# Moving the sums of the weights from GpSimd to VectorE beside the dilated heads and in the second w_up pair, and taking that pair's first two products earlier

## The chip, the cores and the metric

The kernel runs on one core of a Trainium2 chip. The core has five engines that run side by side, each taking its own instructions strictly in order: TensorE (PE: matmuls, with its weight loads shown as PEld), VectorE (DVE), ScalarE (ACT), GpSimd (POOL) and SyncE (SP, which here only issues DMAs). They wait for one another through semaphores. Matmul results land in PSUM, in banks of 128 x 512 floats; everything else lies in SBUF or in device memory. The metric is the device time of one execution in microseconds.

## The reference

One layer of a bidirectional encoder over 1024 sample rows and 256 prompt rows, all in float32, model width 1024:

```python
h = rmsnorm(x, g_mix)
z = h @ w_in                       # queries, keys, values of two branches, and gates
o_a = banded_attention(qa, ka, va, A_WINDOW, 1, rel_bias[:, :8], sink)
o_b = dilated_mixture(qb, kb, vb, rel_bias[:, 8:])   # 3 groups of 4 heads, dilation 1, 4, 16
merged = gates[0] * (o_a @ w_branch_a) + gates[1] * (o_b @ w_branch_b)
x = x + merged @ w_out
h = rmsnorm(x, g_mlp)
x = x + square(relu(h @ w_up)) @ w_down
y = rmsnorm(x, g_final)
```

## The kernel before

**Precision.** Every large product is made of three: each float32 operand is split into a high part (a copy rounded to fp32r, made by ACT) and a low part (operand minus high part, made by DVE, whose tile names end in `lo`), and PE adds low x high, high x low and high x high.

**Seven products for eight.** For the sample rows the projections by w_in and w_up use a Strassen-like scheme: the rows and the contraction are each halved, and so are the columns of a pair of 128-column weight tiles. Seven products (`seven`, twelve matmuls of 128x512 each) take the place of eight. The left factors are A11, A12, S2, S3, S1, A22 and S4, in this order. The right factors are four tiles: `parts[0]`, the split of `raw[0]`, for A11 and A12; `parts[1]`, the split of `ta`, for S2 and S3; `parts[2]`, the split of `tb`, for S1 and A22; `parts[3]`, the split of `raw[1]`, for S4. `ta` and `tb` hold four sums of weight quarters of 128x512 elements, each of which needs the one before it or the raw weights. The 256 prompt rows are multiplied plainly by `parts[0]` and `parts[3]` (`prompt`, 24 matmuls of 128x256).

**Preparing a pair.** `right_pair` is a generator. Step by step it issues the two loads on SP, makes the four sums on POOL (L384 to L387), and splits `raw[0]`, `ta`, `tb` and `raw[1]`, with ACT's half and DVE's half as two steps. With `late=True` the split of `raw[0]` comes ahead of the sums. Its caller decides between which products each step is put (`steps_of(nb, n)` takes the next n steps), and that sets each engine's order: in the stages concerned the instructions run in the order of the program. Tiles with the tag `w` (the weights, their parts, `ta` and `tb`) share ten slots.

**Mixed pairs.** `pair` runs the fourteen pairs of columns of w_in. From the tenth on (j = 9 to 13, `late` there) the attention of the dilated heads (`attention_b`) runs beside the products. `beside` (the function `tick`) is called about every half product and takes two or three attention steps each time: `scores` (PE, then a reduction L518 and a negation L521 on DVE, then exponentials L523 on ACT), `transposes` (PE L534, then a copy), `values_of` (PE L546, a copy, and a store issued by POOL, L550). Pairs 9 to 12 prepare a successor. They issue its loads after S2, and after S1 they take three steps at once: the sums on POOL and the two halves of the split of `raw[0]`.

**The start of w_up.** `up` runs the sixteen pairs of w_up columns. Pair 0 begins while its left factors are still being made: `entering` is advanced by `next(hooks, None)` between products and makes the splits of S3, S1 and A22, then `combine_last` (which makes S4: twice a difference L1390 on DVE, a copy on ACT and a difference L186 on DVE), then `split_prompt` (the tiles phi and plo). S4 and S1 add up in one PSUM bank, `x`: DVE has to read it (`relu2_sum`, L1698) before S4 may add to it. Pair 0 makes its two prompt products after S4, the other pairs make the first of them after A12; all use the single bank `pv`, which ACT empties (L1694, L1695). At the end of each pair POOL makes four sums of the relu outputs (L1753 to L1756), and SP stores seven tiles `u` to memory. Pair 0 takes the load of pair 1's weights after A12, the split of `raw[0]` after S1, and the sums (on POOL) after S4.

Of the kernel before, what the change touches and what calls it, by code (L numbers as in the profile page):

```python
# [15 lines left out]
P = 128  # L16
# [81 lines left out]
def encoder_kernel(  # L98
# [37 lines left out]
    def bank(tag, name=None):  # L136
        return psum.tile([P, 512], F32, name=name or tag, tag=tag, bufs={"mm": 3, "sc": 2, "pt": 2, "pv": 1}[tag])
# [182 lines left out]
    def steps_of(gen, n):  # L320
        for _ in range(n):
            next(gen, None)
# [44 lines left out]
    def right_pair(cols, out, make=wslot, late=False):  # L367
# [12 lines left out]
        if late:  # L380
            yield from part(raw[0], (P, KC, P))
        b11, b21, b12, b22 = raw[0][:, :4], raw[0][:, 4:], raw[1][:, :4], raw[1][:, 4:]
        ta, tb = make("ta", (P, 2, 4, P)), make("tb", (P, 2, 4, P))
        nc.gpsimd.tensor_tensor(tb[:, 0], b12, b11, op=ALU.subtract)  # L384
        nc.gpsimd.tensor_tensor(ta[:, 1], b22, b12, op=ALU.subtract)
        nc.gpsimd.tensor_tensor(ta[:, 0], b22, tb[:, 0], op=ALU.subtract)
        nc.gpsimd.tensor_tensor(tb[:, 1], b21, ta[:, 0], op=ALU.subtract)  # L387
        yield
        if not late:
            yield from part(raw[0], (P, KC, P))  # L390
        for src, shape in ((ta, (P, 2, 4, P)), (tb, (P, 2, 4, P)), (raw[1], (P, KC, P))):
            yield from part(src, shape)
# [419 lines left out]
    if True:  # L812
# [16 lines left out]
        class Rows:  # L829
# [5 lines left out]
            def begin(self):  # L835
                self.z = stage("long", (P, T), n=4)
# [80 lines left out]
        def pair(b, parts, cols, nxt, hooks, beside, late):  # L917
# [6 lines left out]
            nb = right_pair([w_in3[:, :, c : c + P] for c in nxt], np_) if nxt else iter(())  # L924
# [32 lines left out]
            beside()  # L957
            steps_of(nb, 3)
            next(hooks, None)
            seven(z, A22, parts[2], 1, False, mid=beside)  # L960
            one.sum(512, 512, z, c2)
            one.store()
            beside()
            next(hooks, None)
            seven(x, S4, parts[3], 1, False, mid=beside)
            two.direct(0, 512, x)
            beside()
            two.direct(NS, NP, prompt(parts[3], "mm", beside))
# [718 lines left out]
    with ExitStack() as pre:  # L1687
# [12 lines left out]

        def up(j, b, parts, hooks):

# [6 lines left out]
            x, y, z = bank("mm", "x"), bank("pt", "y"), bank("sc", "z")  # L1709
            nb = np_ = None  # L1710
            seven(x, A11, parts[0], 0, last=False)
            c1 = stage("c1", 512)
            nc.scalar.activation(c1, x, AF.Copy)
            steps_of(b, 2)
            next(hooks, None)
            seven(y, A12, parts[0], 1)
# [18 lines left out]
            nc.scalar.activation(c7, z, AF.Copy)  # L1735
            next(hooks, None)
# [71 lines left out]
```

## Time and profile before

| what | value |
|---|---|
| median of 3 runs | 1775.78 us (1774.84 to 1782.72) |
| profiled execution | 1774.43 us |
| its span, first to last instruction | 1772.7 us |
| mean granted TensorE clock | 0.993 |
| POOL sums L384 to L387 | 30 each; 39.8, 42.7, 48.4 and 52.4 us busy |

In the tables of stretches each engine has its busy time and, in parentheses, its number of instructions; PEclk is the share of TensorE's full clock that was granted. In a timeline each row has the start and the length in microseconds, then the engine, the line of the kernel, the operation, the tile written and the tiles read; brackets give how long the engine idled before, and what it seems to have waited for. The chain of waits follows the end of the execution back to its start. The mixed pairs run from about 348 to 585 us, the start of w_up lies near 970 to 1015.

### The profile page before, as it was taken

The numbers are of one execution on the slowest core, as the hardware profiler recorded it, in microseconds if no ns is written. First come the engines' busy times: TensorE is split into PE (matmuls) and PEld (weight loads), VectorE is DVE, ScalarE is ACT, GpSimd is POOL, SyncE is SP. The second block draws the span as 40 slices with busy tenths as digits, with TensorE's granted clock in tenths as the row PEclk, the third lists the DMA queues.
The fourth block names the chain that finished last, engine by engine and source line by source line (L and its number), as shares of the span: only waits on it lengthen the run. The fifth ranks groups of instructions, "written<-read, shape, count | busy, mean of one in ns | idle before, by whom it ended". The sixth has DMA issues, their size and how long they took to land.

```text
span 1772.7 us, 25231 instructions
## 1 busy us (share of the span) xinstructions
PE 1722.8 (97%) x9248; PEld 1461.3 (82%) x9248; DVE 990.1 (56%) x1683; ACT 711.5 (40%) x1531; POOL 550.5 (31%) x472
## 2 busy tenths in 40 slices
PE   7999999999999999999999899999999999999998
PEld 6898888877777899888888688888888788888886
DVE  6623323445545477576648645545454886667575
ACT  6232233344443355464336433333333433333345
POOL 0222321223322365100010355546555451305040
PEclk9999999999999999999999899999999999999999
DMA  6415335555464953185302134443345854633333
GB/s 232 146 38 164 105 112 142 138 164 151 138 169 130 286 144 97 63 273 190 132 36 99 64 126 129 152 151 117 118 146 201 296 191 149 227 101 118 120 113 119
DMA packets 214780, 256.36 MB, mean 145 GB/s; under 512 B 24887, under 2 KB 144523, under 8 KB 214528
## 3 DMA queue, kind: packets, MB, share of 16 engines
q1 hardware_dynamic: 201424, 228.26, 39.9%
q0 software_dynamic: 12144, 24.38, 4.5%
q10 hardware_dynamic: 1088, 2.10, 0.3%
q8 instruction: 73, 1.20, 0.3%
q14 instruction: 51, 0.42, 0.1%
HBM read 169.10 MB, written 90.73 MB: 147 GB/s over the span
## 4 chain that ended last, share of the span: by engine, by line
PE 60%; DVE 3%; ACT 2%; issue 1%; DMA 1%; POOL 0%; SPq 0%; ACTq 0%; DVEq 0%
PE dn L344 20%; PE mm L192 13%; PE x L344 10%; PE pv L344 5%; PE z L344 5%; PE pv L1062 2%; PE y L344 2%; PE pt L1048 1%; PE sc L1025 1%; DMA raw<-in_w_in_dram 1%; PE sc L1026 1%; DVE clo L311 1%; DVE ulo L186 0%; DVE v L1674 0%; DMA scr_g<-z 0%
## 5 line engine op out<-in xcount | busy, mean ns | idle before, releaser
L384 POOL TENSOR_TENSOR tb<-raw 128x512 f32<-128x512 f32 x30 | 39.8, 1326 | 450.0 <-PE mm L192 134.0
L344 PE MATMUL x<-chi,wlo 128*128 128x512 f32 x424 | 170.6, 402 | 7.5 <-ACT phi L185 7.3
L344 PE MATMUL dn<-dhi,ulo 128*128 128x512 f32 x448 | 174.6, 390 | 3.0 <-DVE ulo L186 3.0
L344 PE MATMUL dn<-dlo,uhi 128*128 128x512 f32 x448 | 174.3, 389 | 0.0
L344 PE MATMUL dn<-dhi,uhi 128*128 128x512 f32 x448 | 174.3, 389 | 0.0
L344 PE MATMUL x<-clo,whi 128*128 128x512 f32 x424 | 167.6, 395 | 0.1
L344 PE MATMUL x<-chi,whi 128*128 128x512 f32 x424 | 166.9, 394 | 0.0
L311 DVE TENSOR_TENSOR wlo<-ta,whi 128x1024 fp32r<-128x1024 f32 x30 | 56.6, 1888 | 187.8 <-ACT whi L309 187.8
L311 DVE TENSOR_TENSOR wlo<-raw,whi 128x1024 fp32r<-128x1024 f32 x60 | 93.9, 1564 | 103.7 <-ACT whi L309 103.7
L344 PEld LDWEIGHTS dn<-dhi,ulo 128*128 128x128 f32 x448 | 84.1, 188 | 21.3 <-DVE ulo L186 4.1
L344 PEld LDWEIGHTS x<-chi,wlo 128*128 128x128 f32 x424 | 81.0, 191 | 25.0 <-ACT phi L185 7.7
L186 DVE TENSOR_TENSOR ulo<-uraw,uhi 128x1024 fp32r<-128x1024 f32 x56 | 95.0, 1716 | 11.7 <-ACT uhi L185 11.7
L344 PEld LDWEIGHTS dn<-dlo,uhi 128*128 128x128 f32 x448 | 84.1, 188 | 17.5
L344 PEld LDWEIGHTS dn<-dhi,uhi 128*128 128x128 f32 x448 | 84.1, 188 | 17.4
L344 PEld LDWEIGHTS x<-chi,whi 128*128 128x128 f32 x424 | 80.8, 190 | 17.6
L523 ACT ACTIVATE s<-s,o 128x128 f32<-128x128 f32 (+1 forms) x120 | 52.4, 437 | 103.7 <-issue 58.3
L344 PEld LDWEIGHTS x<-clo,whi 128*128 128x128 f32 x424 | 81.0, 191 | 14.7 <-DVE clo L311 0.4
L1523 POOL TENSOR_TENSOR t<-raw,t 128x1024 f32<-128x1024 f32 x16 | 46.0, 2898 | 142.8 <-DMA raw<-in_w_down_dram 142.8
L1674 DVE TENSOR_TENSOR v<-v,dn 128x512 f32<-128x512 f32 x90 | 59.5, 682 | 43.2 <-PE dn L344 38.9
L344 PE MATMUL dn<-dhi,up 128*128 128x512 f32 x224 | 73.5, 389 | 0.0
L344 PE MATMUL pv<-phi,wlo 128*128 128x256 f32 x256 | 72.5, 283 | 0.9 <-ACT u L1694 0.9
L344 PE MATMUL pv<-plo,whi 128*128 128x256 f32 x256 | 72.6, 283 | 0.0
(332 smaller groups left out, 4785.9 us busy)
## 6 DMA issues: line engine op xcount, KB each, us to landing
scr_u<-u SPq DMA_DIRECT2D x112, 320.0 KB, 2.6
uraw<-scr_u SPq DMA_DIRECT2D x56, 512.0 KB, 4.2
raw<-in_w_in_dram SPq DMA_DIRECT2D x33, 512.0 KB, 5.4
raw<-in_w_up_dram SPq DMA_DIRECT2D x32, 512.0 KB, 5.5
raw<-in_w_down_dram SPq DMA_DIRECT2D x28, 512.0 KB, 6.4
sg<-scr_g SPq DMA_DIRECT2D x32, 256.0 KB, 5.2
uraw<-scr_u SPq DMA_DIRECT2D x28, 256.0 KB, 4.4
v<-scr_v SPq DMA_DIRECT2D x96, 64.0 KB, 2.2
```

The source lines that it names most:

```text
L186: nc.vector.tensor_tensor(lo, src, hi.bitcast(F32), op=ALU.subtract)
L192: nc.tensor.matmul(ps, a, b, start=i == 0, stop=i == len(seq) - 1)
L311: nc.vector.tensor_tensor(lo, src, hi.bitcast(F32), op=ALU.subtract)
L344: nc.tensor.matmul(ps, a, b, start=first and i == 0, stop=last and i == len(seq) - 1, skip_group_check=True)
L384: nc.gpsimd.tensor_tensor(tb[:, 0], b12, b11, op=ALU.subtract)
L523: nc.scalar.activation(s[:, h, :W], s[:, h, :W], AF.Exp, bias=nm[:, h : h + 1], accum_out=l[:, h : h + 1])
L1025: nc.tensor.matmul(ps[:, :W], q, st["k"][1][:, P * lo : P * lo + W], start=True, stop=False)
L1026: nc.tensor.matmul(ps[:, :W], q, st["k"][0][:, P * lo : P * lo + W], start=False, stop=True)
L1048: nc.tensor.transpose(ps[:, P * (i % 4) : P * (i % 4) + P], s[:, h, P * b : P * b + P], ident)
L1062: nc.tensor.matmul(pv[:, HD * h : HD * h + HD], pt[:, 2 * b + h, :], src, start=b == 0, stop=b == W // P - 1)
L1523: nc.gpsimd.tensor_tensor(o, a, b, op=ALU.subtract)
L1674: nc.vector.tensor_tensor(v, v, ps, op=ALU.add)
```

## The change

`right_pair` has a flag `vector` in place of `late`. With it, the split of `raw[0]` comes first and the four sums are made by DVE, one per step. The mixed pairs pass `late` as this flag. There the three steps after S1 are replaced by six, one at each place from after S1 to the middle of the last prompt product, each behind that place's attention steps. In w_up the flag is set for pair 1. Pair 0 takes the split of pair 1's `raw[0]` one product earlier, after S3 and so ahead of `combine_last`. It makes pair 1's products A11 and A12 (`begin`) between its own A22 and S4, and takes the four sums after S4. Pair 1 then starts from the banks that are already filled.

```diff
+        if vector:
+            yield from part(raw[0], (P, KC, P))
         ta, tb = make("ta", (P, 2, 4, P)), make("tb", (P, 2, 4, P))
-        nc.gpsimd.tensor_tensor(tb[:, 0], b12, b11, op=ALU.subtract)
-        nc.gpsimd.tensor_tensor(ta[:, 1], b22, b12, op=ALU.subtract)
-        nc.gpsimd.tensor_tensor(ta[:, 0], b22, tb[:, 0], op=ALU.subtract)
-        nc.gpsimd.tensor_tensor(tb[:, 1], b21, ta[:, 0], op=ALU.subtract)
-        yield
-        if not late:
+        for o, x, y in ((tb[:, 0], b12, b11), (ta[:, 1], b22, b12), (ta[:, 0], b22, tb[:, 0]), (tb[:, 1], b21, ta[:, 0])):
+            (nc.vector if vector else nc.gpsimd).tensor_tensor(o, x, y, op=ALU.subtract)
+            if vector:
+                yield
+        if not vector:
+            yield
             yield from part(raw[0], (P, KC, P))
...
-            nb = right_pair([w_in3[:, :, c : c + P] for c in nxt], np_) if nxt else iter(())
+            nb = right_pair([w_in3[:, :, c : c + P] for c in nxt], np_, wslot, late) if nxt else iter(())
+            def both_(n=1):
+                beside()
+                if late:
+                    steps_of(nb, n)
...
             two.sum(512, 512, x, c7)
-            beside()
-            steps_of(nb, 3)
+            both_()
+            if not late:
+                steps_of(nb, 3)
             next(hooks, None)
-            seven(z, A22, parts[2], 1, False, mid=beside)
+            seven(z, A22, parts[2], 1, False, mid=both_)
...
-            beside()
+            both_()
             next(hooks, None)
-            seven(x, S4, parts[3], 1, False, mid=beside)
+            seven(x, S4, parts[3], 1, False, mid=both_)
             two.direct(0, 512, x)
-            beside()
-            two.direct(NS, NP, prompt(parts[3], "mm", beside))
+            both_()
+            two.direct(NS, NP, prompt(parts[3], "mm", both_))
...
+        def begin(parts):
+            x, y = bank("mm", "x"), bank("pt", "y")
+            seven(x, A11, parts[0], 0, last=False)
+            c1 = stage("c1", 512)
+            nc.scalar.activation(c1, x, AF.Copy)
+            yield
+            seven(y, A12, parts[0], 1)
+            yield x, y, c1
+        begun = {}
...
+            start = begin(parts)
+            if j not in begun:
+                next(start)
+            z = bank("sc", "z")
             steps_of(b, 2)
             next(hooks, None)
-            seven(y, A12, parts[0], 1)
+            x, y, c1 = begun[j] if j in begun else next(start)
             relu2_sum(u11[:, :512], y, c1)
...
             nc.scalar.activation(c7, z, AF.Copy)
+            if not j:
+                steps_of(nb, 2)
             next(hooks, None)
...
-            if nb:
-                steps_of(nb, 3 if j else 2)
+            if nb and j:
+                steps_of(nb, 3)
             seven(z, A22, parts[2], 1, False)
             relu2_sum(u21[:, :512], z, c2)
             next(hooks, None)
+            if not j:
+                *_, begun[1] = begin(np_)
             seven(x, S4, parts[3], 1, False)
             relu2(u12[:, :512], x)
-            if not j:
-                next(nb)
             next(hooks, None)
             if not j:
+                steps_of(nb, 4)
                 prompt_out(prompt(parts[0]), (u11, u21))
```

More of the change, by code (lines that the diff above doesn't have):

```diff
@@ L365, in prompt, with right_pair @@
         return ps
-    def right_pair(cols, out, make=wslot, late=False):
+    def right_pair(cols, out, make=wslot, vector=False):
         raw = [make("raw", (P, KC, P)) for _ in range(2)]
@@ L378, in part @@
             yield from split_steps(*out[-1], src)
-        if late:
+        b11, b21, b12, b22 = raw[0][:, :4], raw[0][:, 4:], raw[1][:, :4], raw[1][:, 4:]
+        if vector:
             yield from part(raw[0], (P, KC, P))
-        b11, b21, b12, b22 = raw[0][:, :4], raw[0][:, 4:], raw[1][:, :4], raw[1][:, 4:]
         ta, tb = make("ta", (P, 2, 4, P)), make("tb", (P, 2, 4, P))
-        nc.gpsimd.tensor_tensor(tb[:, 0], b12, b11, op=ALU.subtract)
-        nc.gpsimd.tensor_tensor(ta[:, 1], b22, b12, op=ALU.subtract)
-        nc.gpsimd.tensor_tensor(ta[:, 0], b22, tb[:, 0], op=ALU.subtract)
-        nc.gpsimd.tensor_tensor(tb[:, 1], b21, ta[:, 0], op=ALU.subtract)
-        yield
-        if not late:
+        for o, x, y in ((tb[:, 0], b12, b11), (ta[:, 1], b22, b12), (ta[:, 0], b22, tb[:, 0]), (tb[:, 1], b21, ta[:, 0])):
[4 more added lines that the diff above has]
+            yield
             yield from part(raw[0], (P, KC, P))
@@ L1708, in up @@
             u11, u12, u22, u21 = u[A11], u[A12], u[A22], u[S3]
-            x, y, z = bank("mm", "x"), bank("pt", "y"), bank("sc", "z")
+            start = begin(parts)
+            if j not in begun:
+                next(start)
+            z = bank("sc", "z")
             nb = np_ = None
-            seven(x, A11, parts[0], 0, last=False)
-            c1 = stage("c1", 512)
-            nc.scalar.activation(c1, x, AF.Copy)
             steps_of(b, 2)
             next(hooks, None)
-            seven(y, A12, parts[0], 1)
+            x, y, c1 = begun[j] if j in begun else next(start)
             relu2_sum(u11[:, :512], y, c1)
```

## The prediction

> **What bounds the kernel now.** I read the page first: TensorE (PE) is busy for almost the whole span, so a gain has to come from places where it idles or is granted less than its full clock.
>
> ```profile
> span 1772.7 us, 25231 instructions
> PE 1722.8 (97%) x9248; PEld 1461.3 (82%) x9248; DVE 990.1 (56%) x1683; ACT 711.5 (40%) x1531; POOL 550.5 (31%) x472
> ```
>
> Then I asked for busy times by stretch, first over the mixed pairs (the dilated heads beside the projection products), then around the start of w_up. Columns: stretch, length, busy time of PE, PEld, DVE, ACT, POOL, granted clock (PEclk), DMA share, GB/s.
>
> ```profile
> 376.00:380.00 4.00, 2.01 (x12) 1.47 (x12) 2.39 (x2) 1.85 (x6) 3.29 (x3) 0.97 0.44 122
> 380.00:384.00 4.00, 4.00 (x16) 3.16 (x16) 3.41 (x13) 1.28 (x7) 1.29 (x3) 0.61 0.14 52
> ...
> 434.00:438.00 4.00, 3.90 (x14) 3.31 (x14) 2.05 (x7) 1.25 (x5) 0.54 (x1) 0.57 0.33 98
> ...
> 442.00:481.00 39.00, 39.00 (x281) 31.91 (x278) 19.51 (x77) 18.96 (x69) 9.07 (x16) 1.00 0.51 147
> ...
> 486.00:490.00 4.00, 2.25 (x9) 1.68 (x10) 3.56 (x14) 1.66 (x8) 2.29 (x2) 0.87 0.15 53
> 490.00:494.00 4.00, 4.00 (x19) 3.20 (x19) 0.98 (x6) 0.76 (x4) 0.98 (x2) 0.70 0.47 123
> ...
> 541.00:545.00 4.00, 4.00 (x26) 3.12 (x25) 3.00 (x11) 2.62 (x10) 0.55 (x1) 1.00 0.37 114
> ...
> 988.00:996.00 8.00, 0.99 (x2) 0.83 (x3) 6.78 (x6) 3.90 (x4) 7.31 (x4) 0.67 0.00 1
> ```
>
> PE is full in the long stretch between (442 to 481: 39.00 of 39.00 us) and empty or slow in short spots near 376, 431, 486, 538 and 990. Each of the five has a run of POOL sums in it. The timelines of POOL, DVE and PE show how the first four arise (start, length, engine, line; in brackets the idle time before).
>
> ```profile
> 376.76 1.26 POOL L386 TENSOR_TENSOR ta<-raw,tb 128x512 f32<-128x512 f32 x1
> ...
> 456.84 0.71 POOL L453 DMA_DIRECT2D bias<-wide  x1
> 457.55 0.73 POOL L454 DMA_DIRECT2D bias<-wide  x1
> ```
>
> ```profile
> 372.12 0.17 DVE L521 TENSOR_SCALAR o<-m 128x2 f32<-128x2 f32 x1
> ...
> 374.46 0.28 DVE L518 CUSTOM_DVE_ANT_0 s<-sc,bias 128x128 f32<-128x128 f32 x1
> ...
> 375.00 3.07 DVE L521 TENSOR_SCALAR o<-m 128x2 f32<-128x2 f32 x1
> ...
> 432.17 1.23 DVE L311 TENSOR_TENSOR wlo<-raw,whi 128x1024 fp32r<-128x1024 f32 x1 [2.16 <-ACT whi L309]
> ...
> 457.07 1.23 DVE L311 TENSOR_TENSOR wlo<-ta,whi 128x1024 fp32r<-128x1024 f32 x1 [1.58 <-ACT whi L309]
> ...
> 481.90 4.71 DVE L311 TENSOR_TENSOR wlo<-raw,whi 128x1024 fp32r<-128x1024 f32 x1 [0.79 <-ACT whi L309]
> ```
>
> ```profile
> 378.69 0.71 PE L534 MATMUL pt<-ident,s 128*128 128x128 f32 x2 [1.94 <-ACT s L523]
> ...
> 430.75 0.33 PE L534 MATMUL pt<-ident,s 128*128 128x128 f32 x1 [0.44 <-ACT s L523]
> ...
> 434.10 1.72 PE L546 MATMUL pv<-v,pt 128*128 128x64 f32 x8 [2.31 <-issue]
> ...
> 486.87 0.69 PE L516 MATMUL sc<-qk 64*128 64x128 f32 x4 [2.19 <-DVE m L518]
> 488.39 0.72 PE L534 MATMUL pt<-ident,s 128*128 128x128 f32 x2 [0.82 <-ACT s L523]
> ...
> 537.70 0.33 PE L534 MATMUL pt<-ident,s 128*128 128x128 f32 x1 [1.98 <-ACT s L523]
> ```
>
> A 0.17 us operation on 2 columns (L521) takes 3.07 us while POOL's sums run: it begins at 375.00 and ends at 378.07, just when POOL's third sum ends (376.76 + 1.26 = 378.02). The reduction L518, with an operand from PSUM, keeps its 0.28 us in the middle of the sums. So DVE operations that work in SBUF alone are held until POOL lets go. Behind them stand the softmax, the transposes and then PE. The 1.23 us split at 481.90 takes 4.71.
>
> **Part A: the sums beside the dilated heads.** Four mixed pairs (j = 9 to 12) prepare a successor, so 16 POOL sums become 16 DVE sums.
>
> What goes. Idle on PE: 1.94, then 0.44 + 2.31, then 2.19 + 0.82, then 1.98: 9.7 us. After three of the four, PE also runs at a low clock: 4.00 x 0.39 + 3.90 x 0.43 + 2.25 x 0.13 + 4.00 x 0.30 = 1.56 + 1.68 + 0.29 + 1.20 = 4.7 us (the clock after the fourth, 541 to 545, is 1.00). Together **14.4 us**. The 2.31 us at 434 isn't held by POOL directly: there the split at 432.17 waited 2.16 us for ACT's copy behind the late softmax, with the copy of the transposes queued behind it. After the change the ACT half and the DVE half of that split are a tick apart, so this should go too.
>
> What comes. A DVE sum of 128x512 stands in no row for SBUF operands alone; its neighbours in size do:
>
> ```profile
> 962.17 0.96 DVE L1379 TENSOR_TENSOR s<-s,hraw 128x768 f32<-128x768 f32 x1
> ...
> 970.32 0.43 DVE L1379 TENSOR_TENSOR s<-s,hraw 128x256 f32<-128x256 f32 x1
> ```
>
> Midway that is 0.69 us, or 2.8 us of DVE work per pair, in a stage where DVE is half busy (19.51 of 39). Each sum comes after its tick's attention step, one per tick. Queued behind it are the next tick's score reduction and copy of transposes, and for those PE waits. Cost between 0 and 16 x 0.69 = 11 us. The nearest row is the split at 457.07: 1.23 us, after waiting 1.58 us, in the same queue in the same sort of tick, inside the stretch in which PE lost nothing. I take 1.5 us in all, since 16 insertions will not all find a gap. ACT issues the same copies, SP the same loads at the same place; POOL's scr_b stores, which were queued behind the sums, go earlier, and nobody waits for them. Net **-12.9 us** (bounds -14.4 and -3.4).
>
> The Trainium skill, "GPSIMD Engine Reference", section "Key points", says that POOL shares its SBUF interfaces with VectorE and contends with DVE instructions in a 2-port mode or with two SBUF inputs. The sums on DVE have two SBUF inputs, so by that rule they could be held by what stays on POOL, its DMA issues. The trace has the split at 457.07, also with two, at its plain 1.23 us while POOL issued the bias loads (456.84 and 457.55), so I add nothing.
>
> **Part B: the start of w_up.** The timelines of PE and DVE and the chain of waits give:
>
> ```profile
> 987.29 0.39 PE L344 MATMUL z<-chi,whi 128*128 128x512 f32 x1
> 995.01 0.77 PE L344 MATMUL x<-chi,wlo 128*128 128x512 f32 x1 [7.34 <-ACT phi L185]
> ...
> 1004.48 0.38 PE L344 MATMUL pv<-phi,wlo 128*128 128x256 f32 x1 [0.87 <-ACT u L1694]
> ```
>
> ```profile
> 985.39 1.22 DVE L1390 TENSOR_TENSOR hraw<-hraw,s 128x1024 f32<-128x1024 f32 x1
> 987.80 1.86 DVE L186 TENSOR_TENSOR clo<-hraw,chi 128x1024 fp32r<-128x1024 f32 x1 [1.19 <-ACT chi L185]
> 989.58 2.28 DVE L1390 TENSOR_TENSOR hraw<-hraw,s 128x1024 f32<-128x1024 f32 x1
> ...
> 994.18 0.68 DVE L1698 TENSOR_TENSOR u<-x,c 128x512 f32<-128x512 f32 x1
> ...
> 1014.67 0.69 DVE L1698 TENSOR_TENSOR u<-y,c 128x512 f32<-128x512 f32 x1 [1.46 <-POOL u L1755]
> ```
>
> ```profile
> 995.01 5.46 PE x L344 x12
> 1000.47 3.16 PE pv L344 x24
> ...
> 1007.62 2.75 PE x L344 x12
> 1010.37 2.72 PE y L344 x12
> 1013.09 2.87 PE pv L344 x24
> ```
>
> PE ends A22 at 987.5 and starts S4 of the first pair at 995.01. S4 adds to bank x, which DVE must first have read (L1698 at 994.18); that read is queued behind combine_last. The ACT phi named as releaser is only what ended last by the clock. S4 then takes 5.46 us, against 2.72 for the same twelve matmuls later, and the prompt product 3.16 against 2.87: the low clock again (0.67).
>
> After the change, on the same time axis. ACT's copy of the second pair's raw[0] follows c7 (at about 984), DVE's split takes 985.4 to 986.6, so A11' and A12' run 987.5 to 993.0 without a wait. combine_last starts 1.2 us later but without POOL beside it: its two held rows fall from 1.86 and 2.28 to 1.22 each, a gain of 1.7. So bank x is free about 0.6 us earlier and S4 starts near 994.4. PE idles about 1.4 us instead of 7.34, and S4 and the prompt product run at full clock (2.74 + 0.29 saved). S4 ends near 997.1. The first prompt product waits about 0.3 for plo, which follows the two sums of relu on DVE; the 0.87 us wait for the one pv bank stays and comes a second time, since no A11' and A12' stand between the prompt products of the two pairs. S2' then starts near 997.1 + 0.3 + 3 x 2.87 + 2 x 0.87 = 1007.7, against 1015.9 now (1013.09 + 2.87): 8.2 us.
>
> Two waits come near. ta is summed by DVE (about 998.5 to 1001.2), copied by ACT after the prompt relus, split near 1007.5: just in time. And relu's sum of u11 waits for POOL's L1755 (1.46 us at 1014.67 now); POOL's chain starts only 3.6 us earlier, with the end of the pair's second prompt product (997.1 + 0.3 + 2 x 2.87 + 0.87 = 1004.0 against 1007.62), so that sum starts near 1011, the split of tb behind it ends near 1014.3, and S1', due at 1007.7 + 2 x 2.72 = 1013.1, stalls about 1.2. The next loads stand on SP behind the stores of u, which gain the same 3.6 us; they are needed a product later than the ones now, so I charge nothing. Net **-7.0 us**, bounds -4 (ta late, and a low clock on S4 after all) and -8.2.
>
> The clock bears on the 1.4 us that remain. Idle of 1.94 us was followed by 0.61 and idle of 1.98 by 1.00, so the length alone doesn't decide; 0.87 at 1004.48 cost nothing. I take no drop. The Trainium skill, "TensorE: Matmul & The Clock Gate", section "Why this matters for your kernels", asks for no idle above about 3 us. By that none of the four spots in the mixed pairs, with single idles of up to 2.31 us, should have slowed, and the sum below would be 4.7 us smaller; the clocks of 0.57 to 0.70 there say otherwise, and the rows decide.
>
> **Sum.** 12.9 + 7.0 = 19.9 us. Both stages sit between others that start from the program's order, and PE is the chain on both sides, so I carry all of it to the end. The profiled execution took 1774.43 us (span 1772.7 plus 1.7): 1774.4 - 19.9 = 1754.5. The median shown is 1775.78, 1.3 above that execution; I put the forecast at **1755**.
>
> **Rivals.**
> 1. *The wait only changes its owner in part A.* DVE's queue is in order: if each sum lands where the softmax has no slack, 0.69 us reach PE 16 times, part A nets 3.4, and the time is 1774.4 - 3.4 - 7.0 = 1764. For it: the transposes follow their scores by a tick or two. Against it: the costless 1.23 us splits. Chance 0.16.
> 2. *Part B gives little.* The pair's S2' waits for ta or S1' for tb, and S4 stays cold: 4 us or less: 1757.5 to 1761. The stalls move a few us later, because POOL's u chain and the single pv bank hold the same order. Chance 0.12, most of it inside my range.
> 3. *DVE becomes the bound beside the heads, and the kernel slower.* Each of the 16 ticks loses its 0.69 us and is followed by a low clock as near 490 (about 1.6 us): 16 x 2.3 = 36.6 against 14.4 + 7.0 saved, 15 us slower, 1790. It decides from 21.4 / 16 = 1.3 us per sum. Against it: DVE is half idle there. Chance 0.04.
> 4. *POOL is not the cause.* If PE's spots came from the pair's own order (ACT's copy ahead of the split), part A would give nothing: 1767.5. Against it: L521's ends coincide with POOL's. Chance 0.08.
>
> The forecast as worked out has 0.60. My range is 1749 (both upper bounds, 1774.4 - 14.4 - 8.2 = 1751.8, and some 3 us for shorter gaps at the same places that I did not count) to 1765 (rival 1). 0.5% is 8.9 us, about what a measurement of this kernel can tell from no change. Faster by more than that (below 1766.9): 0.60 + 0.16 + 0.12 = 0.88; within: 0.08; slower: 0.04.
>
> **What will show it.** Right: no L521 above 0.3 us and no split above 1.3 in the mixed pairs, PE busy for the whole of the four pair ends at clock 1.00; sums of about 0.69 us on DVE; A11' of the second w_up pair before S4, an idle of about 1.4 us ahead of S4, twelve S4 matmuls in 2.7 us, two gaps of 0.87 between three prompt products, and a short gap at S1'. Wrong: PE waiting for ACT's softmax or the copy of transposes just behind a DVE sum; a sum waiting for its ta or tb slot; A11' waiting for its split; or both stages shorter, and the gain lost again before the w_down stage.

## The result and the profile after

| | before | after |
|---|---|---|
| median, lowest to highest | 1776.53 us (1774.84 to 1782.72, 4 runs) | 1754.93 us (1749.7 to 1757.38, 4 runs) |
| profiled execution | 1774.43 us | 1757.38 us |
| its span, granted clock | 1772.7 us, 0.993 | 1755.6 us, 0.996 |

The ratio of after to before is 0.9869, with a 95% interval of 0.9844 to 0.9894. The forecast was 1755.0 us, with a range of 1749 to 1765. The profiled execution of after is the longest of its four, which matters further down.

The page of after, busy time by engine. POOL has 20 instructions less, DVE 20 more:

```profile
PE 1717.7 (98%) x9248; PEld 1457.8 (83%) x9248; DVE 988.3 (56%) x1703; ACT 712.6 (41%) x1531; POOL 519.8 (30%) x452
```

The stretches of after that answer to those shown of before (stretch, length, busy time of PE, PEld, DVE, ACT and POOL with counts, clock, DMA share, GB/s): the four pair ends in the mixed pairs, then the start of w_up, and one stretch at 600 that has no counterpart in the argument so far. PEclk is a mean over the stretch.

```profile
376.00:380.00 4.00, 4.00 (x25) 3.26 (x25) 3.32 (x14) 2.11 (x7) 1.31 (x3) 1.00 0.47 124
380.00:384.00 4.00, 4.00 (x28) 3.20 (x26) 2.34 (x10) 1.76 (x6) 1.78 (x3) 1.00 0.90 247
429.00:434.00 5.00, 5.00 (x36) 4.01 (x35) 3.01 (x13) 1.85 (x6) 0.54 (x1) 1.00 0.62 177
474.00:479.00 5.00, 5.00 (x30) 3.83 (x29) 4.09 (x14) 2.20 (x10) 1.01 (x2) 1.00 0.54 146
524.00:529.00 5.00, 5.00 (x31) 4.01 (x30) 3.93 (x14) 1.66 (x6) 1.08 (x2) 1.00 0.39 113
...
600.00:612.00 12.00, 9.24 (x50) 8.30 (x51) 6.05 (x20) 5.68 (x16) 4.16 (x7) 0.72 0.64 148
...
976.00:984.00 8.00, 6.34 (x29) 4.97 (x28) 5.31 (x6) 4.00 (x4) 0.00 (x0) 1.00 0.00 1
984.00:987.00 3.00, 3.00 (x14) 2.24 (x14) 2.86 (x5) 0.81 (x3) 0.00 (x0) 1.00 0.00 0
```

The four holes in the mixed pairs are closed: PE is full there, at clock 1.00. In the 8 us that end at S4 of the first w_up pair, PE now does 6.34 us of work where it did 0.99.

DVE's groups in after (count, least, median and longest ns, first and last start), with the negation that was held (L521 before, L522 now) and the first of the four sums, then DVE's timeline beside the heads and at the start of w_up (L1398 and L1706 were L1390 and L1698):

```profile
L522 DVE TENSOR_SCALAR o<-m x60: 168/170/229, 357.1 to 552.8; 128x2 f32<-128x2 f32 x60
...
L386 DVE TENSOR_TENSOR tb<-raw x5: 680/684/685, 379.9 to 988.1; 128x512 f32<-128x512 f32 x5
```

```profile
379.83 0.17 DVE L522 TENSOR_SCALAR o<-m 128x2 f32<-128x2 f32 x1
379.91 0.68 DVE L386 TENSOR_TENSOR tb<-raw 128x512 f32<-128x512 f32 x1
380.88 0.42 DVE L264 COPY pt<-pt 128x256 f32<-128x256 f32 x1 [0.29 <-PE pt L535]
...
975.58 1.22 DVE L1398 TENSOR_TENSOR hraw<-hraw,s 128x1024 f32<-128x1024 f32 x1
977.98 1.23 DVE L186 TENSOR_TENSOR clo<-hraw,chi 128x1024 fp32r<-128x1024 f32 x1 [1.19 <-ACT chi L185]
979.12 1.22 DVE L1398 TENSOR_TENSOR hraw<-hraw,s 128x1024 f32<-128x1024 f32 x1
...
982.95 0.68 DVE L1706 TENSOR_TENSOR u<-x,c 128x512 f32<-128x512 f32 x1
```

No negation takes more than 0.229 us (before: up to 3.398), a sum takes 0.68, and DVE has time to spare right behind it: at 380.88 it waits for PE, not PE for it. `combine_last` runs at its plain 1.22 and 1.23 us, where it took 1.86 and 2.28 beside POOL.

PE's timeline in after, at 602 and at the start of w_up (the idle time before a matmul in brackets):

```profile
602.76 1.11 PE L1056 MATMUL pt<-ident,s 128*128 128x128 f32 x4 [3.26 <-ACT pt L262]
...
983.78 0.47 PE L344 MATMUL x<-chi,wlo 128*128 128x512 f32 x1 [1.66 <-DVE u L1706]
...
990.77 0.39 PE L344 MATMUL pv<-phi,wlo 128*128 128x256 f32 x1 [0.87 <-ACT u L1702]
...
994.78 0.38 PE L344 MATMUL pv<-phi,wlo 128*128 128x256 f32 x1 [0.87 <-ACT u L1702]
```

S4 now waits 1.66 us instead of 7.34, and the clock behind it stays at 1.00 (984 to 987). The 0.87 us wait for the one pv bank stands there twice. The hole at 602 is new and belongs to no step of the prediction.

To see where the time went, I take four copies by ACT that both kernels make, as milestones: the copy of S3 in the last mixed pair, the copies of S2 in pairs 0 and 1 of w_up, and the copy of A11 in pair 2. First before, then after:

```profile
579.21 0.60 ACT L951 ACTIVATE c<-z 128x512 f32<-128x512 f32 x1 [1.79 <-PE z L344]
...
980.92 0.59 ACT L1728 ACTIVATE c<-x 128x512 f32<-128x512 f32 x1
...
1018.75 0.60 ACT L1728 ACTIVATE c<-x 128x512 f32<-128x512 f32 x1 [5.85 <-PE x L344]
...
1035.25 0.60 ACT L1713 ACTIVATE c<-x 128x512 f32<-128x512 f32 x1 [1.62 <-PE x L344]
```

```profile
561.33 0.60 ACT L958 ACTIVATE c<-z 128x512 f32<-128x512 f32 x1 [1.79 <-PE z L344]
...
969.97 0.59 ACT L1750 ACTIVATE c<-x 128x512 f32<-128x512 f32 x1
...
1000.95 0.60 ACT L1750 ACTIVATE c<-x 128x512 f32<-128x512 f32 x1 [3.98 <-PE x L344]
...
1018.24 0.60 ACT L1714 ACTIVATE c<-x 128x512 f32<-128x512 f32 x1 [1.62 <-PE x L344]
```

- At the end of the mixed pairs after is 17.9 us ahead. It entered them 0.24 us ahead (334.17 against 334.41 us at the copy before them), so **the mixed pairs give 17.6 us** (12.9 were forecast).
- From the second to the third milestone before takes 37.83 us and after 30.98, a gain of 6.85. The stall at S1' comes only behind that. From the second to the fourth it is 54.33 against 48.27: **the start of w_up gives 6.06 us** (7.0 were forecast). Behind it the lead stays at 17.0 us.
- Between the first and the second, in code that the change doesn't touch, the lead shrinks from 17.9 to 10.95 us: **6.9 us are lost in between**, in this execution. By the copies on the way, 4.6 of them are gone at 611, behind the hole at 602, another 1.6 near 730, and 0.7 from there to 780.

### The profile page after: what moved, and what is told of

Same layout as the page of the kernel before. It is cut to its first block, busy times and chain, and to the rows that moved or that the text cites. A ratio compares the mean times of both kernels' runs of the same rounds, so it can differ in the third digit from the quotient of the medians.

```text
span 1755.6 us, 25218 instructions
## 1 busy us (share of the span) xinstructions
PE 1717.7 (98%) x9248; PEld 1457.8 (83%) x9248; DVE 988.3 (56%) x1703; ACT 712.6 (41%) x1531; POOL 519.8 (30%) x452
## 4 chain that ended last, share of the span: by engine, by line
PE 58%; DVE 4%; ACT 2%; DMA 2%; issue 1%; POOL 1%; SPq 0%; DVEq 0%; ACTq 0%; POOLq 0%
PE dn L344 20%; PE mm L192 13%; PE x L344 9%; PE pv L344 5%; PE z L344 4%; PE pv L1070 2%; PE y L344 2%; PE pt L1056 1%; PE sc L1033 1%; DMA scr_g<-z 1%; PE sc L1034 1%; DVE clo L311 1%; DVE ulo L186 0%; DMA raw<-in_w_in_dram 0%; DMA scr_u<-u 0%
## 5 line engine op out<-in xcount | busy, mean ns | idle before, releaser
L386 POOL TENSOR_TENSOR tb<-raw 128x512 f32<-128x512 f32 x25 | 32.3, 1291 | 358.7 <-PE mm L192 134.7
L344 PEld LDWEIGHTS dn<-dlo,uhi 128*128 128x128 f32 x448 | 84.1, 188 | 17.3
L1778 POOL TENSOR_TENSOR u<-u,u 128x640 f32<-128x640 f32 x16 | 25.6, 1598 | 164.5 <-ACT u L1703 164.5
```

The lines of the kernel that those rows point to most:

```text
L344: nc.tensor.matmul(ps, a, b, start=first and i == 0, stop=last and i == len(seq) - 1, skip_group_check=True)
L386: (nc.vector if vector else nc.gpsimd).tensor_tensor(o, x, y, op=ALU.subtract)
L1778: nc.gpsimd.tensor_tensor(u[S1], u21, u22, op=ALU.add)
```

## The experiments

The theory was that of the prediction: runs of sums on POOL hold DVE, and S4 of the first w_up pair has nothing to cover its wait. Open were whether the engine or the place of the sums matters in each stage, what a sum on DVE costs, and where the 6.9 us went. The table has the first three milestones of every profiled execution: "stretch" is the time from the copy of S3 in the last mixed pair to the copy of S2 in w_up pair 0, "interval" that from there to the copy of S2 in pair 1 (the stall at S1' lies behind it). The last column has how long ACT waited for the loads of the two gate weights that it splits (L231) about 21 and 37 us behind the first milestone (30 in the kernels with earlier loads). Column 3 compares with runs of before on the same chip; products_late to sums_twice ran on another chip than the rest of the experiments.

| kernel | median us (lowest to highest, runs) | ratio to before, 95% | last copy of S3 | stretch | interval | ACT's two waits at L231 |
|---|---|---|---|---|---|---|
| before | 1776.53 (4) | | 579.21 | 401.71 | 37.83 | 2.19, 1.08 |
| after | 1754.93 (1749.7 to 1757.38, 4) | 0.9869 [0.9844, 0.9894] | 561.33 | 408.64 | 30.98 | 3.14, 4.16 |
| heads_only | 1759.16 (1756.84 to 1761.03, 4) | 0.9893 [0.9866, 0.992] | 560.75 | 406.21 | 37.71 | 2.15, 2.58 |
| wup_only | 1770.3 (1768.52 to 1771.99, 6) | 0.9959 [0.9944, 0.9974] | 579.48 | 405.02 | 30.99 | 1.84, 1.97 |
| pool_spread | 1754.71 (1754.24 to 1757.27, 4) | 0.9873 [0.9852, 0.9895] | 561.93 | 404.97 | 30.98 | 2.45, none |
| dve_old_place | 1756.14 (1753.61 to 1759.6, 4) | 0.988 [0.9856, 0.9904] | 565.09 | 403.29 | 30.99 | 2.03, 1.34 |
| products_late | 1758.78 (1754.79 to 1761.09, 4) | 0.9882 [0.9861, 0.9903] | 563.36 | 403.07 | 36.91 | 2.46, 2.15 |
| wup_pool | 1757.49 (1755.71 to 1758.49, 4) | 0.9878 [0.9863, 0.9893] | 561.75 | 402.58 | 34.43 | 2.35, 0.75 |
| early_fetch | 1749.16 (1748.78 to 1749.4, 4) | 0.9832 [0.9817, 0.9847] | 561.74 | 400.86 | 30.66 | 2.40, 0.61 |
| sums_twice | 1753.73 (1 run) | | 561.74 | 402.42 | 30.96 | 2.09, 0.95 |
| after_again | 1752.16 (1752.01 to 1756.65, 5) | 0.9863 [0.9843, 0.9882] | 561.43 | 403.36 | 30.98 | 2.65, 1.27 |
| early_again | 1751.56 (1750.47 to 1753.71, 4) | 0.9854 [0.9836, 0.9873] | 561.38 | 402.15 | 30.68 | 1.94, 0.55 |
| before_early_fetch | 1776.26 (1774.58 to 1780.45, 12) | 0.9999 [0.9989, 1.001] | 580.83 | 402.30 | 36.77 | 2.51, none |
| sums_four | 1762.43 (1 run) | | 574.79 | 400.17 | 30.95 | 2.47, 0.90 |

The runs of before beside them have medians of 1777.66 (heads_only to dve_old_place), 1778.29 (products_late to sums_twice) and 1777.42 us (the rest).

### Each part alone

`heads_only` has the mixed pairs of after and the `up` of before; `wup_only` has the mixed pairs of before and the `up` of after. (The lines of `up` that `heads_only` puts back aren't shown.)

```diff
heads_only, from after
-    def right_pair(cols, out, make=wslot, vector=False):
+    def right_pair(cols, out, make=wslot, vector=False, late=False):
...
-        if vector:
+        if vector or late:
             yield from part(raw[0], (P, KC, P))
...
-        return right_pair([w_up3[:, :, c : c + P] for c in (2 * P * j, 2 * P * j + P)], out, make, j == 1)
+        return right_pair([w_up3[:, :, c : c + P] for c in (2 * P * j, 2 * P * j + P)], out, make, False, j == 1)

wup_only, from after
-            nb = right_pair([w_in3[:, :, c : c + P] for c in nxt], np_, wslot, late) if nxt else iter(())
+            nb = right_pair([w_in3[:, :, c : c + P] for c in nxt], np_) if nxt else iter(())
...
-            both_()
-            if not late:
-                steps_of(nb, 3)
+            beside()
+            steps_of(nb, 3)
```

> Part A alone: DVE sums beside the dilated heads, w_up as before. Theory (POOL's sums hold DVE, and PE waits behind it): ACT's copy of S3 in the last mixed pair, at 579.21 us before and 561.33 in the changed kernel, comes within 1 us of 561.3, a lead of 17.6 us; no L521 above 0.3 us there. The whole gains less than that if the load-bound stretch behind the heads takes some back as it did in the profile of the changed kernel (lead 10.95 us at the start of w_up): 10 to 18 us, ratio 0.990 to 0.994. Rival (the two parts share one gain, for instance through the slots of the weights): less than 8 us.

> Part B alone: mixed pairs as before. Theory (S4 waits for the read of bank x behind combine_last, and the second pair's two products fill the wait): from the copy of S2 in pair 0 to the copy of S2 in pair 1, 37.8 us before, 31.0 in the changed kernel, here 30.5 to 31.5; the whole gains 6 to 8 us, ratio 0.996. Rival (what was won there is late again in w_down): the same 31 us, but a gain below 3 us.

Against the same runs of before, the mixed pairs alone save 1777.66 - 1759.16 = 18.5 us, a little more than the 10 to 18 expected, and the start of w_up alone saves 7.4. The milestones say the same: the mixed pairs end at 560.75 in the one and at 579.48 in the other, the interval is 37.71 and 30.99. The parts don't help or hinder each other: 25.9 us in all, and both together gave 21.6 in the first set of runs and 25.3 (after_again) in another. `wup_only` lost 3.3 us in the stretch (405.02 against 401.71) although its mixed pairs are those of before. So a loss of that size there needs no part A.

### Engine or place in the mixed pairs

`pool_spread` leaves these sums on POOL but puts them one to a tick, as after does. `dve_old_place` makes them on DVE but all at once after S1, in the place and order of before. The lines shown leave out the new parameters and a loop that repeats each sum, once here.

```diff
pool_spread, from after
-            (nc.vector if vector else nc.gpsimd).tensor_tensor(o, x, y, op=ALU.subtract)
+            (nc.vector if vector and not pool else nc.gpsimd).tensor_tensor(o, x, y, op=ALU.subtract)
...
-            nb = right_pair([w_in3[:, :, c : c + P] for c in nxt], np_, wslot, late) if nxt else iter(())
+            nb = right_pair([w_in3[:, :, c : c + P] for c in nxt], np_, wslot, late, True) if nxt else iter(())

dve_old_place, from after
-            (nc.vector if vector else nc.gpsimd).tensor_tensor(o, x, y, op=ALU.subtract)
+            (nc.vector if vector or dve else nc.gpsimd).tensor_tensor(o, x, y, op=ALU.subtract)
...
-            both_()
-            if not late:
-                steps_of(nb, 3)
+            beside()
+            steps_of(nb, 3)
```

> The changed kernel with the mixed pairs' sums back on POOL, but in the new places: the split first, then one sum in each tick. Theory (a run of sums one behind the other is what holds DVE, because POOL lets go only between separate sums): no DVE operation is held for more than about 1.3 us, the length of one sum, and most of the 17.6 us of the mixed stage stays won: lead 12 to 17.6 us at the copy of S3 of the last mixed pair. Rival 1 (any work on POOL costs DVE as much, wherever it stands): lead below 6 us. Rival 2 (only the order counted, POOL holds nothing): lead 17 to 18 us and no L521 above 0.3 us.

> The changed kernel with DVE's sums of the mixed pairs back in the old place: all four in one step after S1, then both halves of the split. Theory (the engine is what counts, the place is second): the four sums take 2.7 us of DVE at once and the split waits for ACT's copy as at 432 us before, so some of PE's idle comes back: lead 8 to 15 us at the copy of S3 of the last mixed pair, with idle of 0.5 to 2 us at each pair end. Rival (the place is what counts): lead below 4 us.

The held operation in `pool_spread`: its group on DVE, and one instance beside POOL's timeline.

```profile
L523 DVE TENSOR_SCALAR o<-m x60: 168/170/1326, 357.2 to 553.4; 128x2 f32<-128x2 f32 x60
...
386.99 0.85 DVE L523 TENSOR_SCALAR o<-m 128x2 f32<-128x2 f32 x1
```

```profile
386.49 1.31 POOL L387 TENSOR_TENSOR ta<-raw,tb 128x512 f32<-128x512 f32 x1
387.88 1.27 POOL L387 TENSOR_TENSOR tb<-raw,ta 128x512 f32<-128x512 f32 x1
```

The hold is still there: a 0.17 us negation takes 0.85 and ends at 387.84, when POOL's sum ends (386.49 + 1.31 = 387.80). POOL still makes some of these sums two in a row, but never three. So the hold now lasts at most one sum (1.326 us at the longest, against 3.398 before), and the ticks have that much to spare: the mixed pairs end at 561.93, within 0.6 us of after. In `dve_old_place` the group and the four sums on DVE are:

```profile
L522 DVE TENSOR_SCALAR o<-m x60: 169/170/235, 357.4 to 556.5; 128x2 f32<-128x2 f32 x60
...
375.46 0.68 DVE L386 TENSOR_TENSOR tb<-raw 128x512 f32<-128x512 f32 x1
...
377.38 0.69 DVE L386 TENSOR_TENSOR tb<-raw,ta 128x512 f32<-128x512 f32 x1
```

No hold is left, but 2.6 us of sums and then the split stand in a row ahead of the next score reduction. PE idles 0.27 to 0.51 us at the pair ends, less than the 0.5 to 2 expected at some of them, and the mixed pairs end at 565.09. They started 0.8 us later than in after, so the packed order costs about 3 us of the 17.6. So in the mixed pairs either half of the change is nearly enough by itself, as far as one profile of each shows. The place alone brings 17.3 us, the engine alone some 14.7. What has to go is the *run* of sums on POOL, and the move to VectorE is one way to do it.

### What a sum on DVE costs

`sums_twice` and `sums_four` issue each of the 16 sums of the mixed pairs two and four times; each ran once.

```diff
-            (nc.vector if vector else nc.gpsimd).tensor_tensor(o, x, y, op=ALU.subtract)
+            for _ in range(times):
+                (nc.vector if vector and not pool else nc.gpsimd).tensor_tensor(o, x, y, op=ALU.subtract)
```

> The changed kernel with each of the 16 sums of the mixed pairs made twice over (the same result): 16 more DVE operations of 0.69 us, two in a row in each tick. Theory (each tick has 1 to 2 us of DVE idle, so a sum costs PE nothing): the copy of S3 of the last mixed pair stays within 2 us of 561.3. Rival (DVE is near its bound there, the sums were just short enough): 5 to 11 us later.

> The changed kernel with each sum of the mixed pairs made four times over (the same result), 2.8 us of DVE work in each tick. Theory (a tick lasts about 3 us and leaves DVE 1 to 2 us): now DVE is the bound in these ticks, and the copy of S3 of the last mixed pair comes 6 to 25 us later than 561.3. Rival (DVE has more room than that): within 3 us.

Doubled, the sums cost nothing: the mixed pairs end at 561.74, against 561.33 and 561.43 in the two profiles of after. Four times as many end at 574.79, 13.5 us later than in after, of which 1.1 were there at the start of the mixed pairs (335.23 against 334.17): they cost 12.4 us, of which some 3.4 are a spell of 6.83 us at half clock that began at 494.06. DVE's and PE's timelines in `sums_four` show how:

```profile
380.50 2.86 DVE L387 TENSOR_TENSOR tb<-raw 128x512 f32<-128x512 f32 x4
```

```profile
386.74 0.91 PE L518 MATMUL sc<-qk 64*128 64x256 f32 x4 [0.80 <-DVE m L520]
```

2.86 us of DVE work in one tick is more than the tick can hide, and PE waits for a score reduction behind it. 2 x 0.69 = 1.4 us is hidden. So the slack of a tick lies between 1.4 and 2.8 us, and the 0.69 us that the change adds is free.

### The start of w_up: products or sums

`products_late` moves A11 and A12 of pair 1 back behind the prompt products, and `wup_pool` keeps the new order but makes pair 1's sums on POOL.

```diff
products_late, from after
-            if not j:
-                *_, begun[1] = begin(np_)
             seven(x, S4, parts[3], 1, False)

wup_pool, from after
-            (nc.vector if vector else nc.gpsimd).tensor_tensor(o, x, y, op=ALU.subtract)
+            (nc.vector if vector and not pool else nc.gpsimd).tensor_tensor(o, x, y, op=ALU.subtract)
...
-        return right_pair([w_up3[:, :, c : c + P] for c in (2 * P * j, 2 * P * j + P)], out, make, j == 1)
+        return right_pair([w_up3[:, :, c : c + P] for c in (2 * P * j, 2 * P * j + P)], out, make, j == 1, j == 1)
```

> The changed kernel with the second pair's first two products back behind the prompt products; the earlier split and DVE's sums stay. Theory (the two products fill the wait for bank x): the wait ahead of S4 is 6 to 7.5 us again, S4 runs at a low clock again, and from the copy of S2 in pair 0 to that in pair 1 it takes 36 to 37.5 us (31.0 in the changed kernel, 37.8 before). The whole is 5 to 7 us slower than the changed kernel. Rival (the gain came from POOL's absence beside combine_last): 31 to 33 us.

> The changed kernel with the second w_up pair's four sums on POOL, the order of all steps kept. POOL has nothing ahead of them, so they run as soon as A22 frees their slots, beside combine_last. Theory (POOL's run of sums holds DVE's operations of combine_last): two of these are stretched to 1.8 to 2.3 us again, S4 starts 1.5 to 2 us later, behind an idle of 3 to 3.6 us, perhaps at a low clock: 32.5 to 35 us from the copy of S2 in pair 0 to that in pair 1 (31.0 in the changed kernel). Rival (the engine doesn't matter here either, as it didn't among the mixed pairs once the sums were spread): 31 us.

In `products_late`, PE's first matmul of S4 and the stretch behind it:

```profile
980.23 0.76 PE L344 MATMUL x<-chi,wlo 128*128 128x512 f32 x1 [7.08 <-DVE u L1706]
```

```profile
980.00:984.00 4.00, 3.77 (x9) 3.03 (x10) 3.83 (x6) 0.57 (x1) 0.00 (x0) 0.50 0.00 0
```

Both the wait (7.08 us) and the low clock (0.50) are back, and the interval is 36.91: of the 6.85 us, 36.91 - 30.98 = 5.9 come from the place of the two products (5.1 of 6.06 if the stall at S1', which it doesn't have, is counted). In `wup_pool` these are POOL, DVE, PE and the stretch behind S4's start:

```profile
970.68 1.64 POOL L387 TENSOR_TENSOR tb<-raw 128x512 f32<-128x512 f32 x1 [92.14 <-PE z L344]
...
975.88 2.13 POOL L387 TENSOR_TENSOR tb<-raw,ta 128x512 f32<-128x512 f32 x1
```

```profile
972.35 2.30 DVE L186 TENSOR_TENSOR clo<-hraw,chi 128x1024 fp32r<-128x1024 f32 x1 [1.19 <-ACT chi L185]
974.57 2.31 DVE L1399 TENSOR_TENSOR hraw<-hraw,s 128x1024 f32<-128x1024 f32 x1
```

```profile
980.32 0.47 PE L344 MATMUL x<-chi,wlo 128*128 128x512 f32 x1 [3.83 <-DVE u L1707]
```

```profile
980.00:984.00 4.00, 3.69 (x11) 2.99 (x12) 3.83 (x6) 1.15 (x2) 0.00 (x0) 0.69 0.00 0
```

POOL has nothing else to wait for here, so its four sums come early and in one run, just beside `combine_last`, whose 1.22 us operations take 2.30 and 2.31. S4 waits 3.83 us instead of 1.66 (3 to 3.6 were expected) and the mean clock of the stretch falls to 0.69: the interval is 34.43, 3.45 more than in after. Here the engine matters, unlike in the mixed pairs. The two parts of the edit overlap, so 5.9 and 3.45 don't add up to 6.85. The whole times bear this out only in their direction: by the ratios to before, products_late is 2 to 3.5 us slower than after, where 5 to 7 were expected, and the intervals overlap.

### The time lost between the stages

In after, ACT takes the split of a gate weight (L231, 1.06 us) in the middle of the banded heads, behind the mixed pairs. If the load isn't there, everything behind it in ACT's queue waits, the copy of transposes included. First ACT's timeline in after, then in after_again:

```profile
599.97 1.06 ACT L231 ACTIVATE whi<-raw 128x1024 fp32r<-128x1024 f32 x1 [4.16 <-DMA raw<-in_w_in_dram]
...
602.13 0.57 ACT L262 ACTIVATE pt<-pt 128x512 f32<-128x512 f32 x1
```

```profile
597.47 1.06 ACT L231 ACTIVATE whi<-raw 128x1024 fp32r<-128x1024 f32 x1 [1.27 <-DMA raw<-in_w_in_dram]
```

That explains the hole at 602 in after: 4.16 us of waiting, the copy of transposes at 602.13, PE at 602.76 after 3.26 us of idling, and a clock of 0.72 over 600 to 612. `early_fetch` and `before_early_fetch` issue these loads one block earlier, in after and in before; `after_again` and `early_again` are after and early_fetch once more, with the same runs of before.

```diff
-                for t0, n in BLOCKS[::2] + BLOCKS[1:2]:
+                for part_, (t0, n) in enumerate(BLOCKS[::2] + BLOCKS[1:2]):
...
                     nc.sync.dma_start(scr_g[c][:, t0 : t0 + n], z[:, :n])
+                    if part_ == 0 and len(raws) < len(PLAIN):
+                        fetch()
```

> The changed kernel, with each load of a plain gate weight (raw) issued one block of products earlier than it is split. Theory (the stretch behind the heads gives back 3 to 7 us because ACT's copy of such a weight waits for its load, 4.16 us at 600 us in the changed kernel, with the copy of the transposes and then PE behind it): no wait of ACT for that load above 1 us, PE's idle of 3.26 us at 602 is gone, and the copy of S2 in w_up's pair 0 comes at 962 to 967 us, against 969.97. The whole gains 2 to 6 us over the changed kernel. Rival (the DMA engines are simply full there, so what comes earlier delays another load): no gain, and a wait of about the same length elsewhere between 570 and 620 us.

> The changed kernel itself once more, for its scatter. Theory (what the load-bound stretch behind the heads gives back differs from run to run with the wait for one load): the copy of S3 of the last mixed pair within 1 us of 561.3 again, but the copy of S2 in w_up's pair 0 anywhere from 962 to 970 us, and single times spread over 5 us or more. Rival (the 7 us given back belong to the change): 969 to 971 us again.

> The changed kernel with the earlier loads of the plain gate weights, again, beside the changed kernel on the same chip. Theory (that wait makes the scatter): faster than the changed kernel by 3 to 7 us, and single times within 3 us of one another. Rival (the first result was a lucky chip): no difference above 2 us.

> The kernel before with the same earlier loads and nothing else. Theory (the wait for the load is a loss of its own, smaller there since ACT waited 1.08 us and PE 0.17 us in the profile of before): 0 to 3 us faster than before. Rival (the earlier loads are worth as much without the change, so that they have nothing to do with what it gave back): 4 us or more faster.

The first result was promising, 1749.16 us and a second wait of 0.61 (the first stayed at 2.40). Repeated beside after itself it was not: 1751.56 against 1752.16 us, where 3 to 7 us had been expected, since after came out shorter this time and early_fetch longer. In before the earlier loads change nothing (0.9999, 0.9989 to 1.001). So the late load explains the hole in that one execution, but no version was shown to be better than after. The 1752.01 to 1756.65 us of after_again are a spread of 4.6 us (at least 5 were expected), and its own profile shows a stretch of 403.36 us, only 1.65 longer than that of before.

Those 1.65 us, and part of the 6.9, come from a second place. PE idles 1.91 us ahead of the transposes of `merged` in all fourteen profiles, before included. First before, then after, each with a matmul 1.2 to 1.6 us later:

```profile
742.93 0.41 PE L1162 MATMUL pt<-ident,merged 128*128 128x128 f32 x2 [1.91 <-DVE oblo L1174]
...
744.12 0.39 PE L192 MATMUL mm<-hhi,whi 128*128 128x512 f32 x1
```

```profile
729.69 0.41 PE L1170 MATMUL pt<-ident,merged 128*128 128x128 f32 x2 [1.91 <-DVE oblo L1182]
...
731.30 0.63 PE L192 MATMUL mm<-hhi,wlo 128*128 128x512 f32 x1
```

The wait is the same, but behind it before keeps its full clock, and in after matmuls of the same shape take 0.63 us instead of 0.39 for a while; that costs 1.6 us. It happens in ten of the fourteen profiles, with and without the change (wup_only and before_early_fetch have it; before, products_late, early_fetch and sums_four don't). So the profile of before was on the lucky side here, and this part of the loss can't be charged to the change.

Over all kernels the stretch takes from 400.17 to 408.64 us, with after at the top. Up to some 45 us behind the first milestone, where both waits for loads lie, the kernels part by -4.6 to +1.2 us from before; the clock behind `merged` adds 1.6 us or nothing, and up to 1.4 us are lost in smaller pieces behind it. In pool_spread the first of the two waits opened a hole in PE (1.66 us at 586.34), in heads_only and after the second. What makes a load late in one execution and not in the next was not settled.

## Why the prediction was right, and where it was not

**Mechanism of part A.** Right. The marks set out in advance are there: no held negation, full pair ends at clock 1.00, sums of 0.68 us. Rival 4 (POOL isn't the cause, the pair's own order is) falls with `dve_old_place`, which keeps that order without POOL and wins 14.7 of the 17.6 us; a part of it survives, in that the packed order costs about 3 us. Rival 1 (the wait changes its owner) falls with `sums_twice`. Rival 3 (DVE becomes the bound) is real but far off: it needed 1.3 us *lost* per sum to make the kernel slower. 1.4 us of DVE work per sum cost nothing, and 2.8 us lost 12.4 / 16 = 0.8 us per sum.

**Size of part A.** 17.6 us against 12.9. Two terms were mis-sized. The step "I take 1.5 us in all, since 16 insertions will not all find a gap" should have been nothing: twice as many insertions found theirs. And the 14.4 us of idle time and low clock was short by about 3 us: by the copies at the pair ends, the four ends give about 3.8, 5.2, 5.2 and 3.3 us, where the rows counted 3.5, 4.4, 4.5 and 2.0. Only about 1 us of that is idle time and low clock that was left out: all gaps of PE between the copies add up to 10.3 us (9.7 counted), and the three spells at half clock, 3.41 us each, to 5.1 (4.7 counted). The other 2 us stand in no idle row and stay open. The 17.6 us lie outside the bounds that the prediction gave this term (3.4 to 14.4).

**Part B.** 6.06 us against 7.0, and most of its steps hold. S4 waits 1.66 us (1.4 forecast) at full clock, `combine_last` runs at 1.22, the pv wait comes twice at 0.87. Rival 2 (4 us or less) falls. PE's start of S1' and the chain of after give the rest:

```profile
1004.13 0.47 PE L344 MATMUL x<-chi,wlo 128*128 128x512 f32 x1 [0.51 <-DVE wlo L311]
```

```profile
983.78 2.99 PE x L344 x12
986.77 3.14 PE pv L344 x24
...
990.77 3.15 PE pv L344 x24
```

S4 and each prompt product take 2.99 and 3.15 us, not 2.72 and 2.87: together some 1.1 us more than forecast, at clock 1.00. So the 3.16 us of the prompt product in before, which the prediction put down to the low clock, need no low clock: ahead of a wait it takes as long at full clock. With the longer wait of S4 the gain at S2' is 6.85 us instead of the 8.2 forecast there. The stall at S1' is 0.51 and takes 0.8 us off, not 1.2, which gives part of that back.

**"I carry all of it to the end."** This step failed in the profiled execution, where 6.9 us were lost behind the heads. It was argued only from the program's order and PE being the chain on both sides, and said nothing of what the loads in between have to spare. In before, PE there is full and the DMA engines too, as this stretch of before shows:

```profile
582.00:602.00 20.00, 19.86 (x112) 17.10 (x110) 3.44 (x8) 1.74 (x3) 6.90 (x11) 1.00 1.00 330
```

A late load there reaches PE through ACT's in-order queue (4.6 us in after), and the clock behind the idle at `merged` took another 1.6. That work arriving 18 us sooner makes the load late isn't shown: after_again and early_fetch arrive as early and lose nothing there, and wup_only, which doesn't, loses 1.7. How much of it shows differs from run to run. 17.6 + 6.06 = 23.7 us would have taken the 1776.5 us of before to 1752.8; the medians of after are 1754.93 and, later, 1752.16. So it is partly luck that the forecast of 1755 came this close: a part A too small, a part B too large, and a loss that wasn't foreseen and isn't the same each time, nearly cancel.

## What to carry to other kernels

When a short VectorE operation on SBUF has a row many times its plain length, look for a run of GpSimd operations beside it: break up the run where other work needs the time in between, or move it to VectorE, after measuring (by doubling it) that a tick has room. Fill an idle wait on TensorE with products whose operands are ready, even from the next pair; the clock lost after the wait goes with it. And when a stage gets shorter, look at the loads of the next one: an engine that waits in order for a late load holds back everything queued behind it. Before such a loss is charged to a change, profile the same kernel twice.

## What the hardware showed

**The hold spans a whole run, not one instruction.** The Trainium skill, "SBUF — State Buffer", section "Who interferes with whom", says that VectorE and GpSimd share a port pair: of two instructions that need it, the one that issues first keeps it for its whole length, while the other fully blocks. `pool_spread` agrees: with single sums the longest hold is 1.326 us, about one sum (1.31). In before it was longer than that. The negation that took 3.07 us began at 375.00, when the first sum was running; POOL's timeline of before goes on with

```profile
375.53 1.28 POOL L385 TENSOR_TENSOR ta<-raw 128x512 f32<-128x512 f32 x1
```

and the sum at 376.76 that the prediction shows. The negation sat through the ends of two sums and came free only after the third. Back to back, the next sum went ahead of the waiting operation. The fourth sum needs the third's result and starts a little behind its end (378.10 against 378.02): that gap is where the negation came free, and the two other long holds of a negation (3.40 us from 426.62, 3.16 from 533.80) ended at the same gap of their runs.

**A short idle can cost the clock, but its length alone doesn't decide.** In the clock records of the fourteen profiles every low spell of these stages is granted 0.50 and lasts 3.41 us or two or three times that; values between, like the 0.69 of wup_pool, are means of windows that hold part of a spell. A spell of 3.41 us costs up to 1.7 us of matmul time. Behind S4's wait there was none after 1.37 to 1.68 us (nine profiles), and one after 3.83, 7.08 and 7.34. But 1.66 us at 586.34 in pool_spread had one behind it, and of the fourteen equal idles of 1.91 us ten had, four had not. That is well under the 3 us of the rule weighed in the prediction, and no threshold comes out of it. The spells of one profile start whole steps of 3.41 us apart (in before at 379.74, 434.35 and 488.96, 16 steps each). The 1.91 us lie within one such step in the ten profiles with a spell, and are spread over two in before (0.53 and 1.38) and sums_four (early_fetch has no spell to tell its steps by). That suggests that the idle time within a step counts, but products_late, with 1.90 us in one step and no spell, speaks against so simple a rule.
